# Hybrid decoder trunk in fp32: wider runs of products in the conv and gate projections, and a later start for the second group of heads

## The chip, the cores and the metric

The kernel runs on one core of a Trainium2 chip. The metric is the device time in microseconds; the time of a kernel is the median over its runs. Its engines are TensorE (PE in the profile, its weight loads PEld), VectorE (DVE), ScalarE (ACT), GpSimd (POOL) and SyncE (SP), which only issues transfers.

## The reference

Two layers on x of 256 tokens by 2048 features, all in float32:

```
h  = rmsnorm(x)
P  = h @ w_in            # columns: q | k | v | gate_B | gate_C | conv_in, 1024 each
A  = differential attention of 8 heads (each two softmaxes of 64 wide q, k), p0 - lam * p1, times v
Cv = gate_B * causal_conv3(gate_C * conv_in)
x  = x + concat(A, Cv) @ w_out
x  = x + relu(rmsnorm(x) @ w_up)^2 @ w_down      # 8192 wide inside
```

## The kernel before

**Precision and products.** Each float32 operand is split into a part hi, rounded to TensorE's faster float32 form, and the rest lo. A product is hi x hi + hi x lo + lo x hi. ScalarE makes hi of a weight tile (whi, L302), VectorE makes lo (wlo, L303), both for tiles of 128 x 1024 read by SP's queue. The pools hold three slots for hi and three for lo, and four for the raw tile.

**The mixer of a layer** runs on TensorE in a fixed order: q, k, v of heads 0 to 3, then of heads 4 to 7 (`linear`, L386), then four times gc and ci, then four gb (`linear_t`, L408: gate_C, conv_in and gate_B, 256 columns of w_in each), then the output projection o. In `linear_t` the weights are the stationary operand. A group takes one weight tile, which holds 4 rows of 128 in k and two halves f of its columns: 8 wide products of 512 columns (whi against hi and lo of the activations at once) and then 8 narrow ones of 256 columns (wlo against hi). A projection is 4 groups. Its two halves in PSUM are joined behind it (`joined`: ACT gc..l, then DVE gc..w), and for gc and ci multiplied and convolved (`conv`: ACT and DVE cv, POOL).

**Attention** is cut in pieces that a list of waiting generators (`Background`) slips between the products. `work.tick()` is a step: each waiting piece counts down, and issues its next part at nought. A head (`unit` in `attention`) has parts: scores (PE sc, L604; then on DVE the bias and maximum L610, on ACT exp L619, on DVE rc, r, c and the weighted difference L630); 10 x pace steps later the transpose of the softmax weights (PE ptp, L635; ACT and DVE pT); 4 x pace steps later the products with v (PE av, L646 and L648; then ACT and DVE ao). Heads of a group begin 8 x pace steps apart. The last head's end normalises the four (DVE an), and 12 x pace steps later the result is transposed back in two pieces two steps apart (PE atp, L677) and written as cat (ACT L681, DVE L682). The pace is 1 for the first four heads, which run beside q, k and v of the second group, and 2 for the second four, which run beside gc and ci. PSUM scores and transposes share one pool, `bank`, of three banks; sc takes two at a time. The order on TensorE is that of the program text; on the other engines a scheduler decides at build time.

`linear` has a step for each k, `linear_t` one after every four products, so 16 for each projection in both.

**The MLP** has, in `up_part` (L955), two tiles taken at once: 16 wide products and 16 narrow ones in a row (upw, upc).

Of the kernel before, what the change touches and what calls it, by code (L numbers as in the profile page):

```python
# [30 lines left out]
KG = 4  # L31
# [74 lines left out]
def trunk(ctx: ExitStack, tc: tile.TileContext, x, w_in, w_out, conv_w, q_norm_g, k_norm_g,  # L106
# [25 lines left out]
    work = Background()  # L132
# [60 lines left out]
    def setup_loads(tile):  # L193

        at = [0]

        def part(rows, n):
            at[0] += n
            return tile[0:rows, at[0] - n:at[0]]

        vec = part(ROWS, P)
        nc.gpsimd.dma_start(vec[0:NCW, :], conv_w.rearrange("l i (k p) -> (l i k) p", p=P))
        for i, g in enumerate((q_norm_g, k_norm_g)):
            for m in range(2):
                nc.gpsimd.dma_start(
                    vec[QG + i * DEPTH:QG + (i + 1) * DEPTH, m * DK:(m + 1) * DK], g)
        nc.gpsimd.dma_start(vec[QG + 2 * DEPTH:MG, :], subln_g)
        nc.gpsimd.dma_start(vec[MG:ROWS, :], mlp_norm_g.rearrange("l (k p) -> (l k) p", p=P))
        lamv = part(1, 4 * DEPTH * DK).rearrange("p (a l d) -> p a l d", a=4, l=DEPTH)
        for i, a in enumerate((lambda_q1, lambda_q2, lambda_k1, lambda_k2)):  # L210
            nc.gpsimd.dma_start(lamv[:, i], a[None])
        sel = part(NB + 1, REL)
        nc.gpsimd.dma_start(sel, selector)
        rel = part(NB + 1, 2 * NH)
        nc.vector.memset(rel[NB:NB + 1, :], NEG)
        nc.gpsimd.dma_start(rel[0:NB, :], rel_bias)
        prod = part(1, 2 * DEPTH * DK).rearrange("p (a l d) -> p a l d", a=2, l=DEPTH)
        return vec, lamv, sel, rel, prod, part(2 * NH, REL)
# [30 lines left out]
    def load_bias(l, bpool, bias, setup):  # L249

        if l == 0:
            yield from small_setup(*setup)
        revs = []
        for j in range(2):
            rev = bpool.tile([P, NH, S], F32, tag="b", name=f"rev{l}{j}")
            src = by_dist_d[j * NH:(j + 1) * NH, 0:S]
            nc.gpsimd.dma_start(
                rev, bass.AP(src.tensor, src.offset, [[1, P], [REL, NH], [1, S]]))
            revs.append(rev)
        yield 4 if l else 12  # L260
        for h in range(0, NH, 2):
            for j in range(2):
                late(nc.scalar.activation(bias[:, j * NH + h:j * NH + h + 2],
                                          revs[j][:, h:h + 2, ::-1], AF.Copy))
            yield 2
# [126 lines left out]
    def linear_t(name, acts, weights):  # L392

        acc = mm.tile([P, 2, 2, S], F32, tag="mm2", name=name)
        nk = len(acts) * KG
        for k0 in range(0, nk, 4):
            hi, lo = weights.take()  # L400
            a = acts[k0 // KG]
            while not a.ready:
                work.tick()
            for part, wt in ((0, hi), (1, lo)):
                for k in range(k0, k0 + 4):
                    for f in range(2):
                        fs = slice(f * P, (f + 1) * P)
                        nc.tensor.matmul(  # L408
                            acc[:, f, 0] if part else acc[:, f], wt[:, k % 4, fs],
                            a.ap[:, 0, k % KG] if part else a.ap[:, :, k % KG],  # L410
                            start=(part == 0 and k == 0), stop=(part == 1 and k == nk - 1),
                            skip_group_check=True)
                    if k % 2:
                        work.tick()
        return acc

# [117 lines left out]
    def q_parts(dst):  # L534


        def put(tp3, gain, c):
            for m, r in enumerate(HALF):
                hi, lo = dst[r, m, :, c], dst[HALF[1 - m], m, :, c]
                nc.scalar.activation(hi, tp3[r], AF.Copy, scale=gain[r])  # L540
                nc.vector.scalar_tensor_tensor(lo, tp3[r], gain[r], hi.bitcast(F32),
                                               op0=ALU.mult, op1=ALU.subtract)
        return put
# [172 lines left out]
    def mixer(l, norm, loads):  # L716

        with ExitStack() as scope:
            biasp = scope.enter_context(tc.tile_pool(name="biasp", bufs=1))
            tmp = scope.enter_context(tc.tile_pool(name="tmp", bufs=3))  # L720
            rpool = scope.enter_context(tc.tile_pool(name="rpool", bufs=RAW))
            bpool = scope.enter_context(tc.tile_pool(name="bpool", bufs=8))
            weights = Weights(rpool)
            setup = None
            if l == 0:
                setup = setup_loads(bpool.tile([P, 2 * KG * S], F32, tag="b", name="setup"))
            for half in range(2):
                for part in range(3):
                    weights.straight(w_in[l], 0, D // P, part * AW + half * CH)
            for q in range(AW // WC):  # L730
                for part in (4, 5):
                    weights.turned(w_in[l], part * AW + q * WC)
            for q in range(AW // WC):
                weights.turned(w_in[l], 3 * AW + q * WC)
            for n in range(D // CH):
                weights.straight(w_out[l], 0, D // P, n * CH)
            loads(weights)

            bias = biasp.tile([P, 2 * NH, S], F32, tag="bias", name="bias")
            work.start(load_bias(l, bpool, bias, setup), 10)  # L740
            hT = norm.tiles
            cat = [Parts(bpool, "b", f"cat{l}{i}") for i in range(4)]
            work.start(norm.factors(), 1)
            kL = biasp.tile([P, 2, 4, S], F32R, tag="kL", name=f"kL{l}")
            for m, r in enumerate(HALF):
                nc.gpsimd.memset(kL[HALF[1 - m], m].bitcast(F32), 0.0)
            for half in range(2):
                h0 = 4 * half
                acc = linear(f"q{l}{half}", hT, weights)
                r = norm.r  # L750
                qT = bpool.tile([P, 2, 4, S], F32R, tag="b", name=f"qT{l}{half}")
                work.start(qk_norm(acc, r, q_parts(qT), q_gain[:, l:l + 1], f"q{l}{half}"))
                acc = linear(f"k{l}{half}", hT, weights)
                kT = bpool.tile([P, 2, 4, S], F32R, tag="b", name=f"kT{l}{half}")
                work.start(qk_norm(acc, r, k_parts(kT, kL), k_gain[:, l:l + 1], f"k{l}{half}"))
                acc = linear(f"v{l}{half}", hT, weights)
                v = bpool.tile([P, 2, NT, CH], F32R, tag="b", name=f"v{l}{half}")
                for t in range(NT):
                    nc.scalar.activation(v[:, 0, t], acc[:, t], AF.Copy, scale=r[:, t:t + 1])
                    nc.vector.scalar_tensor_tensor(v[:, 1, t], acc[:, t], r[:, t:t + 1],  # L760
                                                   v[:, 0, t].bitcast(F32),
                                                   op0=ALU.mult, op1=ALU.subtract)
                work.start(attention(l, qT, kT, kL, v, h0, cat[half], bias, tmp,
                                     1 + half), 3 + 6 * half)
            cv = bpool.tile([P, AW // P, S], F32, tag="b", name=f"cv{l}")
            for q in range(AW // WC):
                acc = linear_t(f"gc{l}{q}", hT, weights)
                u = joined(acc, f"gc{l}{q}")
                nc.gpsimd.tensor_tensor(u, u, norm.bc(2), op=ALU.mult)
                acc = linear_t(f"ci{l}{q}", hT, weights)  # L770
                i = joined(acc, f"ci{l}{q}")
                nc.vector.tensor_mul(u, i, u)
                conv(l, q, u, cv, norm)
            for q in range(AW // WC):
                acc = linear_t(f"gb{l}{q}", hT, weights)
                gate(q, acc, cv, cat[2 + q // 2])

            mnorm = Norm(1, l)
            for n in range(D // CH):
                acc = linear(f"o{l}{n}", cat, weights)  # L780
                for t in range(NT):
                    nc.vector.tensor_add(xs[n][:, t], acc[:, t], xs[n][:, t])
                work.start(mnorm.chunk(n, 2))
        return mnorm
# [483 lines left out]
```

## Time and profile before

| | us |
|---|---|
| median of 3 runs | 2133.86 (2133.83 to 2135.43) |
| the profiled execution | 2133.02 |
| its span, first to last instruction | 2131.2 |
| PE, busy | 2125.1 |
| DVE, busy | 1693.9 |
| ACT, busy | 1349.2 |

A row of the timeline has the start and the length in us, the engine, the line, what is written <- what is read, the shape and the count; in square brackets the idle time of the engine before it and what ended it. A row of the waits has who waited for whom, us in total, how often, and the longest. A row of the windows has the stretch, its length, and for PE, PEld, DVE, ACT and POOL the busy time with the number of instructions, then the granted clock, the share of the DMA engines and GB/s. A row of the groups has busy time and mean ns, then idle time before and its releasers. The starts of products are measured; their ends are modelled.

### The profile page before, as it was taken

How to read it: one execution, taken by the hardware profiler on the slowest of the kernel's cores; microseconds unless marked ns; L12 is line 12 of the kernel's file. 1: busy time of each engine (PE TensorE's matmuls, PEld its weight loads, DVE VectorE, ACT ScalarE, POOL GpSimd, SP SyncE). 2: the span in 40 equal slices, each digit the busy share in tenths (PEclk: the TensorE clock that was granted, in tenths of full speed). 3: DMA queues.
4: the chain of work that ended last, by engine and by line, in shares of the span. 5: the costliest groups of instructions: out<-in, count | busy, mean ns of one | idle time of the engine just before them, and what ended most of it. 6: DMA issues, size and time to landing. Idle time of an engine off the chain costs nothing.

```text
span 2131.2 us, 29207 instructions
## 1 busy us (share of the span) xinstructions
PE 2125.1 (100%) x10925; PEld 1818.4 (85%) x10925; DVE 1693.9 (79%) x2316; ACT 1349.2 (63%) x1776; POOL 165.6 (8%) x226
## 2 busy tenths in 40 slices
PE   9999999999999999999999999999999999999999
PEld 8888888888888888888888888888888888888887
DVE  6778655798888888798766786557988888888986
ACT  6666545677777777656565665446777777675654
POOL 3110100000000000011111101000000000000110
PEclk9999999999999999999999999999999999999999
DMA  8555766677777777788656558656877777777983
GB/s 271 178 166 167 252 193 187 206 252 229 230 236 229 233 235 229 255 297 287 216 170 182 163 162 264 188 178 211 259 231 233 232 235 229 236 229 259 319 297 112
DMA packets 298255, 476.01 MB, mean 223 GB/s; under 512 B 12708, under 2 KB 193782, under 8 KB 298113
## 3 DMA queue, kind: packets, MB, share of 16 engines
q1 hardware_dynamic: 269120, 406.76, 60.5%
q0 software_dynamic: 28800, 67.24, 10.1%
q8 instruction: 85, 1.39, 0.3%
q14 instruction: 58, 0.47, 0.1%
q10 hardware_dynamic: 192, 0.15, 0.0%
HBM read 440.52 MB, written 33.58 MB: 222 GB/s over the span
## 4 chain that ended last, share of the span: by engine, by line
PE 99%; ACT 1%; DVE 0%; issue 0%; DVEq 0%; ACTq 0%
PE upc L955 31%; PE pr L998 14%; PE dn L1079 8%; PE o L386 8%; PE ci L408 4%; PE gb L408 4%; PE k L386 4%; PE q L386 4%; PE v L386 4%; PE gc L408 4%; PE dn L1161 2%; PE dn L998 2%; PE pr1r L998 1%; PE pr0r L998 1%; PE up L955 1%; PE upw L955 1%
## 5 line engine op out<-in xcount | busy, mean ns | idle before, releaser
L303 DVE TENSOR_TENSOR wlo<-raw,whi 128x1024 fp32r<-128x1024 f32 x274 | 343.0, 1252 | 217.8 <-ACT whi L302 213.6
L302 ACT ACTIVATE whi<-raw 128x1024 fp32r<-128x1024 f32 x274 | 290.4, 1060 | 303.3 <-PE o L386 73.6
L955 PE MATMUL upc<-nT,uhi 128*128 128x512 f32 x1920 | 454.7, 389 | 0.0
L955 PEld LDWEIGHTS upc<-nT,uhi 128*128 128x128 f32 x1920 | 360.3, 188 | 74.7
L819 DVE TENSOR_TENSOR ulo<-uraw,uhi 128x1024 fp32r<-128x1024 f32 x256 | 311.9, 1222 | 119.1 <-ACT f L987 91.4
L818 ACT ACTIVATE uhi<-uraw 128x1024 fp32r<-128x1024 f32 x256 | 270.5, 1057 | 159.9 <-PE upc L955 137.5
L955 PEld LDWEIGHTS upc<-nT,ulo 128*128 128x128 f32 x1920 | 246.2, 191 | 9.3
L955 PE MATMUL upc<-nT,ulo 128*128 128x256 f32 x1920 | 249.1, 283 | 0.0
L1079 PE MATMUL dn<-whi,fb 128*128 128x512 f32 x528 | 166.1, 389 | 0.0
L386 PE MATMUL o<-whi,cat 128*128 128x512 f32 x512 | 159.5, 390 | 0.0
L302 ACT ACTIVATE whi<-uraw 128x1024 fp32r<-128x1024 f32 x66 | 70.1, 1062 | 94.0 <-PE dn L1079 77.5
L1079 PEld LDWEIGHTS dn<-whi,fb 128*128 128x128 f32 x528 | 99.1, 188 | 20.6
L844 ACT ACTIVATE b2h<-draw 128x1024 fp32r<-128x1024 f32 x81 | 85.9, 1061 | 45.9 <-PE pr L998 41.3
L386 PEld LDWEIGHTS o<-whi,cat 128*128 128x128 f32 x512 | 96.2, 188 | 19.7
L965 ACT ACTIVATE ev<-upc 128x512 f32<-128x512 f32 x120 | 72.0, 600 | 54.1 <-PE upc L955 54.1
L1079 PE MATMUL dn<-wlo,fb 128*128 128x512 f32 x264 | 102.7, 389 | 0.0
L303 DVE TENSOR_TENSOR wlo<-uraw,whi 128x1024 fp32r<-128x1024 f32 x66 | 80.7, 1223 | 24.8 <-ACT whi L302 24.5
L844 ACT ACTIVATE t24h<-t 128x1024 fp32r<-128x1024 f32 x81 | 86.2, 1064 | 22.2 <-PE pr L998 15.8
L845 DVE TENSOR_TENSOR b2l<-draw,b2h 128x1024 fp32r<-128x1024 f32 x81 | 98.5, 1217 | 1.7 <-ACT b2h L844 1.7
L845 DVE TENSOR_TENSOR t24l<-t,t24h 128x1024 fp32r<-128x1024 f32 x81 | 98.7, 1219 | 1.3
L386 PE MATMUL o<-wlo,cat 128*128 128x512 f32 x256 | 99.6, 389 | 0.0
L845 DVE TENSOR_TENSOR t13l<-t,t13h 128x1024 fp32r<-128x1024 f32 x81 | 98.7, 1219 | 1.1
(408 smaller groups left out, 4153.3 us busy)
## 6 DMA issues: line engine op xcount, KB each, us to landing
uraw<-in_w_up_dram SPq DMA_DIRECT2D x128, 1024.0 KB, 6.2
raw<-in_w_in_dram SPq DMA_DIRECT2D x191, 512.0 KB, 3.8
draw<-in_w_down_dram SPq DMA_DIRECT2D x170, 512.0 KB, 5.2
uraw<-in_w_down_dram SPq DMA_DIRECT2D x66, 512.0 KB, 5.3
raw<-in_w_out_dram SPq DMA_DIRECT2D x64, 512.0 KB, 3.6
hid0p<-f POOLq DMA_DIRECT2D x20, 512.0 KB, 3.6
raw<-in_w_down_dram SPq DMA_DIRECT2D x10, 1024.0 KB, 5.1
fb<-hid0p POOLq DMA_DIRECT2D x20, 512.0 KB, 7.4
```

Source lines behind the costliest of these rows:

```text
L302: pair = (nc.scalar.activation(hi, raw, AF.Copy), nc.vector.tensor_sub(lo, raw, hi.bitcast(F32)))
L303: nc.vector.tensor_sub(lo, raw, hi.bitcast(F32)))
L386: nc.tensor.matmul(acc[:, t], a.ap[:, pa, k % KG, t * P:(t + 1) * P], (hi, lo)[pw][:, j], start=(k == 0 and n == 0), stop=(k == nk - 1 and ...
L408: nc.tensor.matmul(acc[:, f, 0] if part else acc[:, f], wt[:, k % 4, fs], a.ap[:, 0, k % KG] if part else a.ap[:, :, k % KG], start=(part ...
L818: pair = (nc.scalar.activation(hi, src, AF.Copy), nc.vector.tensor_sub(lo, src, hi.bitcast(F32)))
L819: nc.vector.tensor_sub(lo, src, hi.bitcast(F32)))
L844: keep(nc.scalar.activation(hi, src, AF.Copy))
L845: keep(nc.vector.tensor_sub(lo, src, hi.bitcast(F32)))
L955: nc.tensor.matmul(acc[:, 0] if part else acc, wt[part][:, k], a.ap[:, 0, k % KG] if part else a.ap[:, :, k % KG], start=(part == 0 and kh ...
L965: nc.scalar.activation(ev, acc, AF.Copy)
L998: nc.tensor.matmul(prods[n], f[:, pa, a], b[pw], start=(start and m == 0), stop=(stop and m == 2))
L1079: nc.tensor.matmul(prods[p], f[:, pa, 2 * k + t], b[pw][:, n], start=(p in starts and k == 0 and m == 0), stop=(stop and k == 1 and m == 2))
```

## The change

`linear_t` takes two weight tiles at a time: a group is then 16 wide products (8 rows of k by 2 halves) and 16 narrow ones, and a projection has 2 groups. The steps are set anew: of the eight steps for each eight rows of k, six now lie in the wide run (after the rows 0, 2, 3, 4, 6 and 7) and two in the narrow run (after the rows 3 and 7); before, there were two in each of the two wide and two narrow runs. The wait for the activations stands inside the loop over the rows. The second group of heads begins 12 steps after the end of v instead of 9; the first group's 3 steps stay.

```diff
-        for k0 in range(0, nk, 4):
-            hi, lo = weights.take()
-            a = acts[k0 // KG]
-            while not a.ready:
-                work.tick()
-            for part, wt in ((0, hi), (1, lo)):
-                for k in range(k0, k0 + 4):
+        for k0 in range(0, nk, 8):
+
+            tiles = [weights.take() for _ in range(2)]
+            for part in range(2):
+                for k in range(k0, k0 + 8):
+                    a = acts[k // KG]
+                    while not a.ready:
+                        work.tick()
+                    wt = tiles[(k - k0) // 4][part]
                     for f in range(2):
                         fs = slice(f * P, (f + 1) * P)
                         nc.tensor.matmul(
...
-                    if k % 2:
+                    if k % 4 == 3 or (part == 0 and k % 2 == 0):
                         work.tick()
...
                 work.start(attention(l, qT, kT, kL, v, h0, cat[half], bias, tmp,
-                                     1 + half), 3 + 6 * half)
+                                     1 + half), 3 + 9 * half)
```

## The prediction

> **What bounds the kernel now.** I read the page first (busy time and the chain), then TensorE's waits, then its timeline in the two mixers, and only then the timelines of VectorE (DVE) and GpSimd (POOL).
>
> ```profile
> span 2131.2 us, 29207 instructions
> PE 2125.1 (100%) x10925; PEld 1818.4 (85%) x10925; DVE 1693.9 (79%) x2316; ACT 1349.2 (63%) x1776; POOL 165.6 (8%) x226
> PE 99%; ACT 1%; DVE 0%; issue 0%; DVEq 0%; ACTq 0%
> ```
>
> TensorE is busy for the whole span and carries 99% of the chain. The ends of products are modelled, so I count by starts below. What matters is whether TensorE ever waits; the view of its waits has two lines:
>
> ```profile
> PE sc L604 <- DVE cat L682: 1.2, 2, 0.6
> PE warm L160 <- DVE mhalf L152: 1.1, 1, 1.1
> ```
>
> The second is the start of the program. The first is two waits of 0.6 us, one per layer: the scores of the second group of four heads wait until VectorE has read a transposed piece of the first group out of its PSUM bank. So a change to the order of TensorE's work can gain only these waits and whatever its own products cost above their floor, and it can lose without limit if it makes TensorE wait elsewhere.
>
> **Runs of sixteen.** Today a projection alternates eight wide products (512 columns) with eight narrow ones (256). The gate projection of layer 0 runs undisturbed, and the MLP's second pair already has runs of sixteen:
>
> ```profile
> 255.86 2.00 PE L408 MATMUL gb<-nT,whi 128*128 128x512 f32 x8
> 257.70 1.11 PE L408 MATMUL gb<-nT,wlo 128*128 128x256 f32 x8
> 258.65 2.00 PE L408 MATMUL gb<-nT,whi 128*128 128x512 f32 x8
> ...
> 300.55 0.40 PE L386 MATMUL o<-whi,cat 128*128 128x512 f32 x1
> ...
> 402.55 3.82 PE L955 MATMUL upw<-nT,uhi 128*128 128x512 f32 x16
> 406.20 2.08 PE L955 MATMUL upw<-nT,ulo 128*128 128x256 f32 x16
> 408.12 3.82 PE L955 MATMUL upw<-nT,uhi 128*128 128x512 f32 x16
> 411.77 2.08 PE L955 MATMUL upw<-nT,ulo 128*128 128x256 f32 x16
> 413.68 3.82 PE L955 MATMUL upc<-nT,uhi 128*128 128x512 f32 x16
> ```
>
> The gate stage is 4 projections of four 8+8 groups: (300.55 - 255.86) / 16 = 2.793 us for one, 5.586 for two. A 16+16 group takes (413.68 - 402.55) / 2 = 5.565. The difference is 0.021 us for each change of width and back that goes. A projection has two such groups instead of four 8+8, and there are 12 projections in each of 2 layers: 48 x 0.021 = **1.0 us** less. The count of products, weight loads and splits is unchanged.
>
> The Trainium skill, TensorE: Matmul & The Clock Gate, section Back-to-back issue gap, gives an isolated product a gap that follows from its own width alone, with nothing for the width of its neighbour. By it this term would be nought and the sum 1.0 us smaller. The 0.021 us above speak against it, though they compare two different lines of the kernel; that is the first rival.
>
> **Second heads three steps later.** The rows around the wait, TensorE first, then VectorE:
>
> ```profile
> 156.06 1.98 PE L408 MATMUL gc<-nT,whi 128*128 128x512 f32 x8
> ...
> 161.11 0.64 PE L408 MATMUL gc<-nT,wlo 128*128 128x256 f32 x4
> 161.59 0.60 PE L677 MATMUL atp<-ident,an 128*128 128x128 f32 x4
> ...
> 162.50 1.09 PE L408 MATMUL gc<-nT,whi 128*128 128x512 f32 x4
> 163.43 0.22 PE L604 MATMUL sc<-kT,qT 128*128 128x128 f32 x1
> 164.26 0.38 PE L604 MATMUL sc<-kT,qT 128*128 128x256 f32 x1 [0.61 <-DVE cat L682]
> ...
> 165.18 1.09 PE L408 MATMUL gc<-nT,whi 128*128 128x512 f32 x4
> ...
> 176.37 0.39 PE L604 MATMUL sc<-kT,qT 128*128 128x128 f32 x2
> ...
> 177.28 1.07 PE L408 MATMUL ci<-nT,whi 128*128 128x512 f32 x4
> ```
>
> ```profile
> 161.66 1.23 DVE L303 TENSOR_TENSOR wlo<-raw,whi 128x1024 fp32r<-128x1024 f32 x1 [1.08 <-ACT whi L302]
> 162.80 0.75 DVE L760 SCALAR_TENSOR_TENSOR v<-v,rowf,v 128x512 fp32r<-128x512 f32 x1
> 163.47 0.74 DVE L682 SCALAR_TENSOR_TENSOR cat<-atp,s_gain,cat 128x512 fp32r<-128x512 f32 x1
> ```
>
> The first head's scores last 165.18 - 163.43 = 1.75 us, the second head's 177.28 - 176.37 = 0.91: the wait costs 0.84, and with its twin in layer 1 **1.7 us**. In the built order of the changed kernel that head stands after the first 16+16 group, ten wide products of the next, and the two transposed pieces. One piece costs (162.50 - 161.11) less the 0.95 of eight undisturbed narrow products (258.65 - 257.70), so 0.44. A wide product is (406.20 - 402.55) / 16 = 0.228. The head begins at 156.06 + 5.57 + 2.28 + 0.88 = 164.8, 1.4 us later than now. Its second bank came free at 163.47 + 0.74 = 164.21. The built order on VectorE also puts that read ahead of the second eviction of v instead of behind it (163.47 - 162.80 = 0.67 sooner), so I expect the bank at 163.5 to 164.2: the wait goes entirely. Next late is the bank of the second transposed piece, but nothing asks for that before the first transpose of softmax weights (ptp), which now comes at 180.08. The head's own products stay; v is wanted only by the products behind that transpose.
>
> **The pieces' new places.** Steps stay at eight per eight rows of k, so all later pieces keep their distance in steps. Of the pieces, nine in a layer now stand where a narrow run ends instead of inside a wide run, or so I count in the built order (four transposes of weights, four products with v, one transpose of the result). The trace has no such place. From both sides:
>
> ```profile
> 179.15 1.09 PE L408 MATMUL ci<-nT,whi 128*128 128x512 f32 x4
> 180.08 0.49 PE L635 MATMUL ptp<-ident,s 128*128 128x128 f32 x3
> 180.32 1.18 PE L408 MATMUL ci<-nT,whi 128*128 128x512 f32 x4
> 181.34 1.10 PE L408 MATMUL ci<-nT,wlo 128*128 128x256 f32 x8
> ...
> 186.01 0.28 PE L646 MATMUL av<-v,pT 128*128 128x256 f32 x1
> ```
>
> Behind a transposed piece four wide products take 181.34 - 180.32 = 1.02 instead of 0.91, a refill of 0.11. If the new place hides that refill for all 18 pieces, 2.0 us go as well; if it adds a second one, 2.0 us come. But the piece as a whole is hardly dearer in a wide run (181.34 - 179.15 - 8 x 0.228 = 0.37 for three transposes) than in a narrow run (0.44 for four), so I take **nought** and keep both ends for the range.
>
> **Weights two at a time.** A group now holds two of the three slots for hi and for lo. Nothing moves on SP's or POOL's queue (same order in the built program), and the splits cost what they cost:
>
> ```profile
> L303 DVE TENSOR_TENSOR wlo<-raw,whi 128x1024 fp32r<-128x1024 f32 x274 | 343.0, 1252 | 217.8 <-ACT whi L302 213.6
> L302 ACT ACTIVATE whi<-raw 128x1024 fp32r<-128x1024 f32 x274 | 290.4, 1060 | 303.3 <-PE o L386 73.6
> ```
>
> The tightest tile is the second of the next group. Its hi slot is free after 8 wide products (1.83 us into the group), its lo slot after 16 wide and 8 narrow (3.65 + 0.95 = 4.60). It is used at 5.57 + 1.83 = 7.40 and 5.57 + 4.60 = 10.17. Less the splits of 1.06 and 1.25 the lead is 4.5 and 4.3 us, so this costs nothing; three such groups follow each other at 402.55, 408.12 and 413.68 without a gap. The cover goes if ACT or VectorE falls over 4 us behind.
>
> **The new order on VectorE.** In the built order each head's four score additions are followed by two weight splits, and on the heads that meet a projection's end its join (0.7 us) also stands ahead of the weights' pT, which the products with v need. Behind a waiting split stand rc, c and pT, and TensorE waits for pT at the product with v.
>
> ```profile
> 173.03 1.76 DVE L303 TENSOR_TENSOR wlo<-raw,whi 128x1024 fp32r<-128x1024 f32 x1 [0.76 <-ACT whi L302]
> 175.78 1.23 DVE L303 TENSOR_TENSOR wlo<-raw,whi 128x1024 fp32r<-128x1024 f32 x1 [0.98 <-ACT whi L302]
> ...
> 181.24 0.18 DVE L622 RECIPROCAL rc<-su 128x4 f32<-128x4 f32 x1 [0.53 <-ACT s L619]
> ...
> 181.79 0.55 DVE L638 TENSOR_TENSOR pT<-ptp,pT 128x384 fp32r<-128x384 f32 x1
> ...
> 184.05 0.68 DVE L422 TENSOR_TENSOR ci00w<-ci,ci00l 128x512 f32<-128x512 f32 x1
> ```
>
> ```profile
> 172.42 1.29 POOL L769 TENSOR_TENSOR gc00w<-gc00w,rowb 128x512 f32<-128x512 f32 x1 [22.30 <-DVE gc00w L422]
> ```
>
> ```profile
> 182.30:195.40 13.10, 13.10 (x83) 11.68 (x82) 11.77 (x28) 8.66 (x22) 1.29 (x1) 1.00 0.53 160
> ```
>
> Now pT is ready at 182.34 and used at 186.01, 3.7 us ahead. After the change, counted from a head's start: scores 0.91, six wide products 1.37, sixteen narrow 1.91 make 4.2, where the second split may start; it ends at 5.5; the join 0.68, rc, r and c with the 0.55 from rc's start to pT's, and pT with 0.55 make 7.3. The product with v stands one group after the transpose: 4.2 + 0.37 + 5.57 = 10.1. The lead is 2.8 us, an estimate, enough for no cost. VectorE is busy for 11.77 of 13.10 us there, so a lag is worked off slowly. A split that meets a POOL product is longer: 1.76 against 1.23 us, with POOL until 173.71. The Trainium skill, SBUF — State Buffer, section SBUF: two separate sides, says that a VectorE operation with two SBUF inputs and a reading GpSimd operation take turns at one port pair, the loser waiting in full; the 0.53 us agree. Two such meetings would take the lead down, not away.
>
> **The sum.** 1.0 + 1.7 + 0 = 2.7 us less: a span of 2128.5 for 2131.2. The profiled execution took 2133.02 (1.8 around the span), the median of the runs is 2133.86; on that scale 2133.86 - 2.7 = **2131.2 us**, 0.13% less. About 0.2% (4.3 us) is what a measurement of this kernel can tell from no change.
>
> **The rivals.** (1) The runs buy nothing, since the 0.021 us belong to other lines: only the wait goes, 2132.2. Against it: the same widths in both. Chance 0.08. (2) The wait stays, moved: VectorE reads the bank no sooner than the head arrives, as its splits now wait for lo slots that come free later. Only the runs gain: 2132.9. For it: 164.8 against 164.2 is a thin margin. Chance 0.10. (3) Slower: VectorE's queue. Two splits that wait for narrow products ahead of rc and pT push pT past the product with v. There are 8 such products, four in each layer. The gain is used up when pT slips by 2.8 + 2.7 / 8 = 3.1 us on each, and 0.2% is lost from 2.8 + 7.0 / 8 = 3.7 us; a slip of 3.8 gives 2131.2 + 8 x 1.0 = 2139.2. For it: the 90% in the row above, and no row shows two waiting splits there today. Against it: the lead left is more than two whole splits. Chance 0.10. (4) The refills vanish at the new places: 2131.2 - 2.0 = 2129.2, just over 0.2% faster. Chance 0.10. That the change doesn't do what it says is out: the built order shows runs of sixteen and the shifted heads.
>
> **How the numbers follow.** The forecast has 0.62; with rivals 1 and 2 the chance within 0.2% is 0.80, faster 0.10 (rival 4), slower 0.10 (rival 3). The range goes from half of rival 4 (2129.6) to no gain at all (2133.9), which takes in rivals 1 and 2, and leaves out rival 3 and the rest of rival 4.
>
> **What would show it.** In the changed profile: no wait of sc on cat in TensorE's waits; the first head's scores 0.9 us long and begun near 164.8; a gate stage of 44.5 us instead of 44.69; no new line in TensorE's waits. Wrong: av waiting for pT, gc, ci or gb waiting for a split, or a gate stage as long as before.

## The result, and the profile after

The changed kernel takes **2138.25 us** (median of 12 runs, 2135.86 to 2143.19) against 2133.49 us for the kernel before in the same sessions (12 runs, 2132.70 to 2135.43): a ratio of 1.0023 with a 95% interval of 1.0016 to 1.0031. It is slower, where 2131.2 us and no measurable difference were forecast. The profiled execution took 2136.23 us with a span of 2134.4 us; that of before took 2133.02 and 2131.2.

Three lines of the page after answer to those shown of before:

```profile
span 2134.4 us, 29223 instructions
PE 2125.1 (100%) x10925; PEld 1818.9 (85%) x10925; DVE 1685.8 (79%) x2316; ACT 1351.0 (63%) x1776; POOL 161.0 (8%) x226
PE 99%; DMA 1%; ACT 0%; DVE 0%; DVEq 0%; issue 0%; ACTq 0%
```

TensorE's busy time is the same to a tenth, so the 3.2 us of longer span are waiting, and the chain now has a per cent of DMA. TensorE's waits name the place:

```profile
PE ci L410 <- ACT whi L302: 4.4, 3, 2.1
PE warm L160 <- DVE mhalf L152: 1.1, 1, 1.1
```

The wait of the scores on cat is gone, as forecast. In its stead a content projection waits for a hi part. TensorE's timeline of the changed kernel shows the good part first, then the bad one, then the end of the gate stage (a last row of a stretch counts only the products inside the stretch that was asked for, as x11 of 16):

```profile
164.68 0.39 PE L606 MATMUL sc<-kT,qT 128*128 128x128 f32 x2
...
165.60 1.55 PE L410 MATMUL gc<-nT,whi 128*128 128x512 f32 x6
...
231.59 2.68 PE L410 MATMUL gc<-nT,whi 128*128 128x512 f32 x11
...
249.38 2.12 PE L410 MATMUL ci<-nT,whi 128*128 128x512 f32 x8
253.61 2.12 PE L410 MATMUL ci<-nT,whi 128*128 128x512 f32 x8 [2.11 <-ACT whi L302]
255.57 2.07 PE L410 MATMUL ci<-nT,wlo 128*128 128x256 f32 x16
257.48 1.78 PE L410 MATMUL gb<-nT,whi 128*128 128x512 f32 x7
...
302.01 0.40 PE L386 MATMUL o<-whi,cat 128*128 128x512 f32 x1
```

The first head's scores begin at 164.68 and last 0.92 us (forecast 164.8 and 0.9). The gate stage lasts 302.01 - 257.48 = 44.53 us (forecast 44.5, before 44.69). But in the last content projection, ci3, the wide run breaks after its eighth product, at 249.38 + 8 x 0.228 = 251.20, and goes on at 253.61, 2.4 us later. Layer 1 has the twin of it at 1314.57. The view has 2.1 us where the starts have 2.4, since it counts from the modelled end of the last product; the sums below go by starts.

The tile that ci3 waits for is split by ScalarE (ACT) as soon as its transfer lands. Its row in the kernel before, then in the changed one:

```profile
251.46 1.06 ACT L302 ACTIVATE whi<-raw 128x1024 fp32r<-128x1024 f32 x1 [3.09 <-DMA raw<-in_w_in_dram]
```

```profile
252.50 1.06 ACT L302 ACTIVATE whi<-raw 128x1024 fp32r<-128x1024 f32 x1 [3.17 <-DMA raw<-in_w_in_dram]
```

In both ScalarE has been idle for 3 us, and what it waits for is a transfer, not a slot. Before, the part was ready at 252.52 and TensorE wanted it at 253.06:

```profile
253.06 2.00 PE L408 MATMUL ci<-nT,whi 128*128 128x512 f32 x8
```

So the kernel before had 0.54 us in hand there, and no view of TensorE's waits could show it. SP's timeline says why a transfer is late at this place; before, then after:

```profile
232.92 3.56 SPq L811 DMA_DIRECT2D uraw<-in_w_up_dram  x3
236.57 3.93 SPq L343 DMA_DIRECT2D raw<-in_w_in_dram  x1
240.54 1.23 SPq L811 DMA_DIRECT2D uraw<-in_w_up_dram  x1
241.87 18.85 SPq L343 DMA_DIRECT2D raw<-in_w_in_dram  x9
```

```profile
233.40 3.89 SPq L813 DMA_DIRECT2D uraw<-in_w_up_dram  x3
237.39 2.93 SPq L343 DMA_DIRECT2D raw<-in_w_in_dram  x1
240.37 1.30 SPq L813 DMA_DIRECT2D uraw<-in_w_up_dram  x1
241.76 17.76 SPq L343 DMA_DIRECT2D raw<-in_w_in_dram  x8
```

The MLP's first four weight tiles (uraw, 1 MB each, 128 x 2048 in float32) are fetched in the middle of the mixer's own weight tiles (raw, half as large). The windows, before and then after, have the DMA engines full while they run (last two columns: share of the DMA engines, GB/s):

```profile
221.00:233.00 12.00, 12.00 (x72) 10.63 (x71) 7.53 (x8) 5.82 (x12) 4.45 (x6) 1.00 0.56 177
233.00:245.00 12.00, 12.00 (x74) 10.60 (x73) 8.53 (x11) 5.73 (x9) 2.28 (x1) 1.00 1.01 327
```

```profile
233.00:245.00 12.00, 12.00 (x74) 10.66 (x73) 9.26 (x13) 5.16 (x7) 1.97 (x2) 1.00 0.95 303
245.00:257.00 12.00, 9.88 (x57) 8.20 (x56) 4.65 (x5) 5.39 (x6) 0.60 (x1) 1.00 0.95 332
```

When this burst may begin is told by the waits of SP's queue in 215 to 262 us; before, then after:

```profile
SPq L811 <- DVE an L668: 1.0, 1, 1.0
```

```profile
SPq L813 <- DVE an L670: 0.8, 1, 0.8
```

It waits for VectorE's `an`, the normalised second heads, whose end frees the memory that uraw takes. VectorE's timeline around `an`, before, after, and in a kernel with the late start alone (the first experiment below):

```profile
231.54 1.29 DVE L668 TENSOR_TENSOR an<-ao,af 128x512 f32<-128x512 f32 x2
```

```profile
226.88 0.42 DVE L654 TENSOR_TENSOR ao<-av,ao 128x256 f32<-128x256 f32 x1
230.89 1.23 DVE L303 TENSOR_TENSOR wlo<-raw,whi 128x1024 fp32r<-128x1024 f32 x1 [3.58 <-issue]
232.03 1.29 DVE L670 TENSOR_TENSOR an<-ao,af 128x512 f32<-128x512 f32 x2
```

```profile
229.28 1.23 DVE L303 TENSOR_TENSOR wlo<-raw,whi 128x1024 fp32r<-128x1024 f32 x1 [1.99 <-ACT whi L302]
230.90 1.29 DVE L668 TENSOR_TENSOR an<-ao,af 128x512 f32<-128x512 f32 x2 [0.39 <-POOL af L664]
```

With the late start alone `an` begins when GpSimd has its factor, at 230.90. In the changed kernel a lo split stands idle at the head of VectorE's queue until 230.89, with `an` behind it; GpSimd's factor is ready at 230.89 there too, so the split's own 1.14 us are what `an` loses. The row names no releaser. The split's lo slot comes free when eight narrow products of the run before are done, and in a run of sixteen those come late: they start at 229.68 and are done at about 230.6 (8 x 0.119 us). The experiment with eights in ci2 alone tests it.

**The account of one layer**, by starts in layer 0. The tile is ready 252.52 - 232.92 = 19.60 us after the first uraw before, 253.56 - 233.40 = 20.16 after. The first uraw is issued 0.30 us behind the start of the gate_C projection gc3 before (232.62), and 233.40 - 231.59 = 1.81 behind it after. And ci3 asks for the tile 253.06 - 232.62 = 20.44 us after gc3's start in runs of eight, 19.46 in runs of sixteen (the changed and late kernel below), since eight narrow products that came ahead of it now come behind. In hand: 0.54 - 0.98 - 1.51 - 0.56 = -2.5 us, where the trace has a wait of 2.4. Of the 1.51, 0.30 come with the late start alone (0.60 in the table below) and 1.21 with the runs. Why the burst itself took 0.56 longer isn't shown.

The tile isn't issued late on its own account. In both kernels it stands right behind the fourth uraw in SP's queue and lands about 1.4 us after it: before, the fourth uraw takes 9.4 us to land from 240.54 and the tile 9.5 from 241.87; after, both take 10.6, from 240.37 and 241.76. So what is late is the burst.

### The profile page after: what moved, and what is told of

The parts are those of the page before. It is cut to its first block, busy times and chain, and to the rows that moved or that the text cites. A ratio compares the mean times of both kernels' runs of the same rounds, so it can differ in the third digit from the quotient of the medians.

```text
span 2134.4 us, 29223 instructions
## 1 busy us (share of the span) xinstructions
PE 2125.1 (100%) x10925; PEld 1818.9 (85%) x10925; DVE 1685.8 (79%) x2316; ACT 1351.0 (63%) x1776; POOL 161.0 (8%) x226
## 4 chain that ended last, share of the span: by engine, by line
PE 99%; DMA 1%; ACT 0%; DVE 0%; DVEq 0%; issue 0%; ACTq 0%
PE upc L957 31%; PE pr L1000 14%; PE dn L1081 8%; PE o L386 8%; PE gb L410 4%; PE gc L410 4%; PE k L386 4%; PE v L386 4%; PE q L386 4%; PE ci L410 4%; PE dn L1163 2%; PE dn L1000 2%; PE pr1r L1000 1%; PE pr0r L1000 1%; PE up L957 1%; PE upw L957 1%
## 5 line engine op out<-in xcount | busy, mean ns | idle before, releaser
L303 DVE TENSOR_TENSOR wlo<-raw,whi 128x1024 fp32r<-128x1024 f32 x274 | 332.4, 1223 | 225.5 <-ACT whi L302 162.9
L1081 PEld LDWEIGHTS dn<-whi,fb 128*128 128x128 f32 x528 | 99.1, 188 | 20.6
```

Source lines behind the costliest of these rows:

```text
L303: nc.vector.tensor_sub(lo, raw, hi.bitcast(F32)))
L1081: nc.tensor.matmul(prods[p], f[:, pa, 2 * k + t], b[pw][:, n], start=(p in starts and k == 0 and m == 0), stop=(stop and k == 1 and m == 2))
```

## The experiments

The theory after this reading: the wait is a transfer behind the burst, made late by two things, a tile asked for 1 us sooner and a burst begun 1.2 to 1.5 us later. Rivals: it is the second heads' later start; it is the order of SP's queue; it is one of the two things alone. "Stall" below is the stretch from gc3's start to the first gate projection's, less 23.2 us, which it takes undisturbed (253.06 + 2.79 - 232.62 before).

**Each half of the change alone.** The changed kernel with the old start, and the kernel before with the new one:

```diff
-                                     1 + half), 3 + 9 * half)
+                                     1 + half), 3 + 6 * half)
```

> The changed kernel with the second heads begun 9 steps after v as before (runs of sixteen alone). Theory T (transfers): in the third quarter of the mixer four 1 MB loads of w_up go ahead of the last loads of w_in on SP's queue, and a run of sixteen needs the second tile's hi 0.93 us sooner and frees its slots later, so TensorE waits in the last conv_in projection. By T that wait stays (4 to 5 us in both layers together), and the wait of the first scores on cat may come back (up to 1.7 us): 2136 to 2140 us. Rival S (the start): the later heads delay the w_up loads and with them all behind; without the later start the wait in conv_in is gone: 2132 to 2133 us.

```diff
-                                     1 + half), 3 + 6 * half)
+                                     1 + half), 3 + 9 * half)
```

> The kernel before with the second heads begun 12 steps after v, runs of eight kept. T: only the wait of sc on cat goes, 1.7 us in both layers: 2131.5 to 2132.0 us, no wait in conv_in. S: a wait in conv_in appears, 2135 us or more.

The runs alone: 2143.45 us (2141.91 to 2143.86), ratio 1.0044 [1.0031, 1.0056]. The start alone: 2131.63 us (2130.99 to 2133.33), ratio 0.9993 [0.9984, 1.0002], 1.6 us below 2133.25 for before, which is the 1.7 forecast for it. That interval reaches past 1, so by the times alone the gain isn't clear of noise; the trace has it (the wait of the scores is gone, and 0.79 us a layer by starts, below). So the start does no harm by itself, and the loss comes with the runs. They are even worse without the start, beyond the 2140 us that were expected at most. TensorE's waits, SP's timeline and VectorE's row of `an` in the runs alone:

```profile
PE ci L410 <- ACT whi L302: 7.0, 2, 4.0
PE sc L606 <- DVE cat L684: 1.0, 2, 0.5
```

```profile
231.91 6.37 SPq L813 DMA_DIRECT2D uraw<-in_w_up_dram  x4
238.38 23.64 SPq L343 DMA_DIRECT2D raw<-in_w_in_dram  x9
```

```profile
230.51 1.29 DVE L670 TENSOR_TENSOR an<-ao,af 128x512 f32<-128x512 f32 x2 [2.38 <-POOL af L666]
```

This kernel waits in another way. `an` stands behind no split here, and the burst isn't late: the first uraw is issued 0.18 us before gc3 starts (232.09). But the build put all four uraw ahead of the raw tile that is ci3's second, which the changed kernel issues at 232.14, ahead of its burst. TensorE now waits for that tile, 4.0 us in layer 0, and the stall as defined above is 5.8 and 6.0 us, the lower clock that the last section shows included. So a tile that the build's order puts behind the burst can cost more than a late burst, and the two causes below are those of the changed kernel, not of every build with runs of sixteen.

**The burst out of the way.** The first four uraw are issued where the text has them, behind all of the mixer's weights, once in the changed kernel and once in the kernel before:

```diff
-                        nc.sync.dma_start(
+                        load = nc.sync.dma_start(
...
+                        if i < 2:
+                            late(load)
```

> The changed kernel with the first four w_up loads kept behind the last w_out load on SP's queue, so that none of them meets the w_in loads. T: the wait in conv_in goes in both layers, the rest of the forecast holds: 2130.5 to 2131.5 us, little spread. Rival Q (the two tiles held, or the order on VectorE and ScalarE, and not the transfers): the wait stays, 2136 us or more.

> The kernel before with the same four loads kept behind the last w_out load. T: nothing waited there in the kernel before (0.5 us in hand), so the time stays within 0.5 us of 2133.5. If the later loads themselves cost something in the MLP's first stage, it shows here as a loss.

Changed and late: 2141.89 us (2140.17 to 2143.86). Before and late: 2144.34 us (2142.61 to 2145.80). Loading late costs 2144.34 - 2133.25 = 11 us of its own in the kernel before, as the MLP then waits for its first tile (waits of the two, changed first) and TensorE's clock can fall after such a wait, of which more in the last section. So both expected times were missed by over 10 us:

```profile
PE up L959 <- ACT uhi L822: 6.2, 2, 3.1
```

```profile
PE up L957 <- ACT uhi L820: 6.2, 2, 3.1
PE sc L604 <- DVE cat L682: 1.2, 2, 0.6
```

But no line of ci is left in the changed one, and with this price on both sides it is 2144.34 - 2141.89 = 2.45 us shorter than the kernel before with it. The five runs of each spread over 3 us and their clocks differ (0.997 to 0.999), so the figure is rough. The starts are surer: from gc0 to the output projection a layer takes 143.36 us changed and 144.48 before, 2.24 us less in two layers, where the forecast had 2.7. TensorE's timeline of the changed and late kernel gives the undisturbed times:

```profile
231.04 1.32 PE L410 MATMUL gc<-nT,whi 128*128 128x512 f32 x5
...
248.67 3.82 PE L410 MATMUL ci<-nT,whi 128*128 128x512 f32 x16
```

Its ninth product is at 248.67 + 1.83 = 250.50, 19.46 us after gc3's start: the demand used above.

**The other queue.** The four uraw of the changed kernel go through GpSimd's queue, so that none of them stands ahead of a raw tile on SP's:

```diff
-                        nc.sync.dma_start(
+                        (nc.gpsimd if i < 2 else nc.sync).dma_start(
```

> The changed kernel with the four early w_up loads of each layer issued on GpSimd's queue instead of SP's, at about the same time. If the w_in loads are late because they stand behind the w_up loads in one queue (T-queue): they land sooner, the wait in conv_in shrinks or goes, 2131 to 2133 us. If the DMA engines' bandwidth alone decides (T-bandwidth): the wait of conv_in stays near 2 us a layer, 2135 us or more. GpSimd's own products for the convolution come later in either case.

2136.12 us (2134.16 to 2139.76), ratio 1.0013 [1.0004, 1.0022]; GpSimd's timeline and TensorE's waits:

```profile
234.28 3.61 POOL L813 DMA_DIRECT2D uraw<-in_w_up_dram  x4 [2.99 <-PE gc L410]
```

```profile
PE ci L410 <- ACT whi L302: 5.6, 2, 2.8
```

The wait stays, 2.8 us a layer. The burst begins 0.5 us later here (234.28 - 231.99 = 2.29 us after gc3's start), which can account for the longer wait. A raw tile issued on SP's queue at 238.11, with no uraw ahead of it in that queue, took 15.1 us to land. So in the changed kernel the wait doesn't come from standing behind the burst in one queue: the transfers share the DMA engines, whichever of the two queues they come from.

**Sooner or later.** Five kernels have runs of eight in some projections and of sixteen in the others, all with the late start. `linear_t` gets an argument for the number of tiles (1 or 2), and the calls differ; for the first of them:

```diff
-                acc = linear_t(f"gc{l}{q}", hT, weights)
+                acc = linear_t(f"gc{l}{q}", hT, weights, 1 if q == 3 else 2)
...
-                acc = linear_t(f"ci{l}{q}", hT, weights)
+                acc = linear_t(f"ci{l}{q}", hT, weights, 1 if q == 3 else 2)
```

Eights in gc3 and ci3, where the wait is:

> The changed kernel, but the last gate_C and conv_in projections of each layer (the two that stand where the four w_up loads are under way) in runs of eight; 20 of 24 projections in runs of sixteen, second heads 12 steps after v. Theory T (the w_in loads behind the w_up loads land late, and runs of sixteen ask for them sooner): no wait of conv_in on whi, the sc wait gone: 2133.3 - 1.7 - 40 x 0.021 = 2130.8 us, little spread. Rival H (slots held two at a time by the projections ahead delay the loads as well): a wait of conv_in on whi stays, 1 us or more a layer: 2132.5 us or more, with spread.

Sixteens in the gate stage alone:

> Second heads 12 steps after v, runs of sixteen in the gate_B projections alone. T and H: no wait, 2133.3 - 1.7 - 16 x 0.021 = 2131.3 us, 0.3 below the kernel with the later start alone (2131.63). If the first gate_B projection still asks for late loads, a wait of gb on whi shows.

Sixteens in ci3 alone:

> Second heads 12 steps after v, runs of eight everywhere except the last conv_in projection of each layer. In the kernel with the later start alone the last tile's hi was ready at 251.73 and used at 252.11 in layer 0, 0.4 us in hand; in a run of sixteen it is asked for 0.93 us sooner. If only this decides (T-sooner): a wait of about 0.5 us a layer, 2132 to 2133 us. If the slots held by all the projections ahead make the difference (H), nothing of it shows here beyond that; if the wait is 2 us as in the changed kernel, the holding ahead plays no part.

Eights in ci2, gc3 and ci3:

> The changed kernel with three of its projections, the ones with the third and fourth widest demand on weights while the feed-forward part's first four 1 MB loads run (content of batch 2, content of batch 3 and gate of batch 3 ahead of it), back in runs of eight; all others in runs of sixteen and the second heads begun at step 12, as in the changed kernel. Theory (two halves of one wait: the run of sixteen in the last content projection asks for its second weight tile 0.96 us sooner, and the runs of sixteen ahead of it hold VectorE's split of the weights, and behind it the normalised second heads, whose end frees the memory that the four loads take, 1.2 us longer): both halves go, the loads begin 0.6 us after the gate projection of batch 3 as with eights everywhere, the wait of the last content projection is under 0.4 us in both layers together, and the time is that of the late start alone, 2131.6 us, less 36 narrow widths' changes at 0.021 us, 0.8 us: 2130.9 us. Rival (the runs elsewhere delay the split in another way): the loads still begin 1.8 us after the gate projection, a wait of 1 us or more a layer stays, and the time is 2133 us or more.

Eights in ci2 alone:

> The changed kernel with one projection alone, the content of batch 2, in runs of eight; the last gate and the last content projection stay in runs of sixteen. Theory (the delay of the normalised second heads behind a split that waits for a slot of the low parts is half of the wait): with that projection in eights the heads end sooner, the four loads begin about 0.6 us after the gate projection of batch 3 and not 1.8, and the wait of the last content projection falls from 2.2 us a layer to between 0.4 and 1.0; the time falls from about 2136 us to between 2131.5 and 2133. Rival (only the sooner demand counts): the wait stays at 2 us a layer or more and the time at 2135 us or more.

| kernel | uraw begins after gc3's start (layers 0, 1) | ci3 in runs of | stall, us (layers 0, 1) | median, us | ratio |
|---|---|---|---|---|---|
| late start alone | 0.60, 0.60 | 8 | 0, 0 | 2131.63 | 0.9993 [0.9984, 1.0002] |
| sixteens in the gate stage | 0.61, 0.62 | 8 | 0.7, 0 | 2131.77 | 0.9992 [0.9983, 1.0001] |
| eights in ci2, gc3, ci3 | 0.60, 0.61 | 8 | 0.3, 1.0 | 2131.96 | 0.9991 [0.9982, 1.0000] |
| sixteens in ci3 alone | 0.61, 0.62 | 16 | 1.0, 0.5 | 2132.86 | 1.0001 [0.9992, 1.0009] |
| eights in ci2 alone | 0.60, 0.60 | 16 | 1.8, 1.3 | 2133.21 | 0.9998 [0.9989, 1.0006] |
| eights in gc3 and ci3 | 1.81, 1.81 | 8 | 1.7, 1.9 | 2134.85 | 1.0007 [0.9998, 1.0016] |
| the change | 1.81, 1.81 | 16 | 2.7, 2.8 | 2138.25 | 1.0023 [1.0016, 1.0031] |

The waits of three of them, in the order eights in gc3 and ci3, eights in ci2 alone, eights in all three:

```profile
PE ci L410 <- ACT whi L302: 2.4, 3, 1.1
```

```profile
PE ci L410 <- ACT whi L302: 2.5, 2, 1.5
```

```profile
PE ci L410 <- ACT whi L302: 0.7, 1, 0.7
```

The two kernels of which the first expects no wait, with eights in gc3 and ci3 and with sixteens in the gate stage, both have one: in the first the burst is still late, and the second differs from the late start alone only behind ci3, so that its 0.7 us show how far the landing scatters from one execution to the next.

Both causes are there, and each can be taken away without the other. The demand alone (sixteens in ci3 alone) stalls 1.0 and 0.5 us, the late burst alone (eights in gc3 and ci3) 1.7 and 1.9, both together 2.7 and 2.8. The medians, which rest on 11 or 12 runs each, go the same way: 1.2, 3.2 and 6.6 us above the late start alone. With gc3 and ci3 back in eights the stall is 0.9 to 1.0 us a layer shorter, as much as the demand is later, but the burst stays at 1.81. With ci2 alone back in eights, the projection ahead of gc3, the burst goes to 0.60 in both layers: it is the run of sixteen in ci2 that holds the lo slot, the split and `an`. VectorE's timeline of the kernel with eights in all three has `an` behind GpSimd's factor again:

```profile
229.01 1.23 DVE L303 TENSOR_TENSOR wlo<-raw,whi 128x1024 fp32r<-128x1024 f32 x1 [1.99 <-ACT whi L302]
230.63 1.29 DVE L670 TENSOR_TENSOR an<-ao,af 128x512 f32<-128x512 f32 x2 [0.39 <-POOL af L666]
```

The sizes were expected finer than they came. With ci2 alone in eights 0.4 to 1.0 us a layer and at most 2133 us were expected, and 1.3 to 1.8 and 2133.21 came; with all three in eights under 0.4 in both layers together, and 1.3 came. The hi part of ci3's last tile is ready anywhere from 19.0 us (late start alone, layer 1) to 20.6 us (eights in all three, layer 1) after the first uraw, so one profile can't split the two causes to better than that scatter. The shortest three (2131.63 to 2131.96) all have eights in ci2, gc3 and ci3; they lie 1.4 to 1.8 us below before, each with an interval that reaches or passes 1.0000, and the runs elsewhere add nothing to the late start that their medians could show.

## Why the prediction was wrong

**The step that failed** is "Weights two at a time". It found the tightest tile's lead to be 4.5 and 4.3 us "so this costs nothing", counting when the slots of hi and lo come free. The split needs the raw tile too, and at ci3 the tile isn't there: ScalarE's row had 3.09 us of idle time ended by a transfer, and the lead was 0.54 us. The example of three groups that follow each other without a gap (402.55 to 413.68) lies in a stretch where the tiles are early. The step also says that "Nothing moves on SP's or POOL's queue (same order in the built program)". The order did stay; the times moved, by 1.51 us against TensorE, and only the times matter where a transfer lands 0.54 us ahead of its use. The step put its term at nought; it measured 2.7 and 2.8 us, 5.5 in the two layers.

**The new order on VectorE** was weighed for pT alone. No product with v waits for pT, so rival 3 in its own form did not come. But its mechanism, a waiting split with something behind it, did: behind it stood `an`, and behind `an` 4 MB of transfers. Among what would make it wrong the prediction named a ci waiting for a split; no chance stood on it. That the 2138.25 us lie close to rival 3's 2139.2 is luck, as the path to them is another.

**What held.** The scores' wait went, so rival 2 is out. By the starts of projections, the kernel with the late start alone has gc0 0.83 and ci0 0.08 us shorter than before and the four projections behind them 0.12 longer: 0.79 a layer, 1.6 in all for 1.7 forecast. **The runs** were worth 0.16 us a layer in the gate stage, where 8 x 0.021 = 0.17 was forecast, so the 0.021 holds and rival 1 is out. In the eight projections beside attention they gave 0.17 a layer instead of 0.34 (0.02 + 0.02 in gc0 and ci0, 0.09 in the next four, 0.04 in the last two). Whether the pieces' new places cost that 0.17 wasn't tried; neither end of the 2.0 us on **the pieces' places** came near, and rival 4 is out.

The span adds up: -1.6 for the start, -2 x 0.33 for the runs, +2.7 + 2.8 for the stalls make +3.3, and it grew by 3.2. On that scale the median would be 2133.49 + 3.2 = 2136.7. The other 1.5 us come with a lower granted clock: 1.000 in the runs of 2135.86 to 2136.99 us, 0.998 and 0.999 in those of 2137.42 to 2139.89, 0.997 in 2141.55 and 2143.19, and 1.000 in the 69 runs of the kernel before that were taken beside the experiments. A thousandth of 2134 us is 2.1 us, so by this estimate the lower clock is large enough for it.

## What to carry to other kernels

Before an order is changed, look for inputs that arrive just in time: rows of the splitting engine whose idle time is ended by a DMA, and windows where the DMA share is 1.0; TensorE's waits show none of it while half a microsecond is in hand. A lead counted from free slots holds only where the data is already on the chip. And for a split that may wait longer, follow everything behind it in its queue to the end: here a normalisation, the memory that it frees, and a burst of transfers that then falls on the next stage's weights.

## What the runs showed of the hardware

A wait of TensorE can cost more than its length. TensorE's timeline of the runs alone in layers 0 and 1, and the windows in layer 0:

```profile
250.13 2.72 PE L410 MATMUL ci<-nT,whi 128*128 128x512 f32 x8 [4.03 <-ACT whi L302]
...
1313.64 3.78 PE L410 MATMUL ci<-nT,whi 128*128 128x512 f32 x8 [2.98 <-ACT whi L302]
```

```profile
250.00:255.00 5.00, 4.87 (x20) 4.37 (x21) 2.80 (x3) 3.25 (x4) 0.00 (x0) 0.66 0.57 171
```

Behind the 4.03 us the granted clock is 0.66 over 5 us. The last two wide products of that row start 427 ns apart instead of 228, and all but the first of layer 1's, behind 2.98 us. The 2.4 us in the profiled run of the change did nothing of the kind (granted clock 1.00 in 253 to 257 us). Behind 3.1 us the clock halved in both layers of the changed kernel with late loads, but in one layer only of the kernel before with them, where the first eight products take 2.12 us in layer 0 and 3.61 in layer 1:

```profile
393.37 2.12 PE L957 MATMUL up<-nT,uhi 128*128 128x512 f32 x8 [3.10 <-ACT uhi L820]
...
1456.70 3.61 PE L957 MATMUL up<-nT,uhi 128*128 128x512 f32 x8 [3.09 <-ACT uhi L820]
```

The Trainium skill, TensorE: Matmul & The Clock Gate, section What's actually happening, has the array's clock fall to half after an idle window of about 3.4 us, a window that runs freely and doesn't begin anew with the kernel. The factor agrees roughly, as 427 / 228 is 1.87. The length doesn't: waits of 2.98 and 3.09 us, counted from modelled ends, are shorter than such a window and halved the clock. A window that runs freely may be why the same 3.1 us went both ways, but no run here shows it. The same may lower the clock in some of the change's runs, but none of those was profiled, so this stays open.

The DMA engines didn't serve one queue ahead of the other: with the burst on GpSimd's queue the raw tiles on SP's were as late as behind it on one queue (5.6 us of waits against 4.4, with a burst begun 0.5 us later). One of them took 15.1 us to land, against 3.3 to 4.8 us for the 14 that the kernel before issues in 170 to 215 us, where no uraw is under way.
